# When background sums are queued: two weight units behind their split, the second half with the second group, none ahead of a half-step's last tile

## The chip, the cores and the metric

The kernel runs on one core of one Trainium2 chip. The metric is the device time of one execution in microseconds (us), as the median of several runs. A profile of one execution shows every instruction of the core's engines: TensorE (PE; its weight loads are listed as PEld), VectorE (DVE), ScalarE (ACT), GpSimd (POOL) and SyncE (SP), which issues most of the DMAs.

## What is computed

Two layers of an encoder trunk over 512 tokens of 1024 features, in f32. Each layer has three half-steps, so six follow one another, numbered s = 0 to 5: an FFN (s = 0, 3), a mixer of three parallel head groups (s = 1, 4), and a second FFN (s = 2, 5). Each is conditioned on one vector c:

```python
c_act = jax.nn.silu(c)
for l in range(DEPTH):
    mod = (c_act @ ada_w[l] + ada_b[l]).reshape(b, N_SUB, 3, 1, D_MODEL)

    h = modulate(x, mod[:, 0, 0], mod[:, 0, 1])          # x * (1 + scale) + shift
    y = swiglu_ffn(h, ffn1_w_in[l], ffn1_w_out[l])       # (silu(gate) * up) @ w_out, d_ff 2816
    x = layer_norm(ALPHA * x + 0.5 * mod[:, 0, 2] * y, ln_g[l, 0], ln_b[l, 0])
    ...
```

The change is about `c_act @ ada_w`: for each half-step a shift, a scale and a gate of 1024 numbers, each the product of one vector of 1024 with a 1024 x 1024 block of weights (4 MB). Shift and scale of a half-step are needed when its input is made, the gate when its output is added to x.

## The kernel before, in words

**The main work.** x lies in four tiles of 128 tokens (`xt`). For the matmuls its normalised and modulated transpose lies as features by tokens in `hT`, split in a high part `hh` and a low part `hl`, so that three fast matmuls (`mm3`, L106: low x high, high x low, high x high) stand for one f32 matmul. Weights are split in the same way: SP loads a unit of 1 MB (`ri`, `ro`), ACT copies it to the high part (`hi`, `ho`), and DVE subtracts for the low part (`li`, `lo`).

`ffn` (L659) goes through 11 pairs of 256 features in two groups, 0 to 5 and 6 to 10. A pair `jp` needs two weight units, gate and up; each is followed by a call of `tick()`. Then come its 4 x 8 x 3 = 96 matmuls into four PSUM banks (`pf`), then silu, product and split into `ah`, `al`. After a group, `out_proj` (L710) multiplies its 12 or 10 slices with the output weights, in two halves of 512 columns (`h`), each with up to three weight units and a `tick()` behind each; all ticks of a half precede its matmuls (`po`). The second group's second half goes tile by tile: 30 matmuls for token tile 0, `fold` (adds the gated result to x), layer norm, then `drain()` (L391), then tile 1, and from there on `modulate(s + 1, t - 1)` for the tile before. So tiles 0 to 2 of the next half-step's input are made there. The last tile, 3, is made inside the next half-step: in an FFN, `last_tile` is called behind the second of eight groups of matmuls of the first pair (`POS`, L681), which run first on tokens 0 to 255 and then on 256 to 511. Its `hl` is two DVE instructions, one for each half of the features.

**The background work** makes gates, scales and shifts with generators that are advanced by ticks. One part (a gate, a scale or a shift) consists of:

- `ada_acc` (L227): eight loads of rows (`ra`, 512 KB, from two buffers, `adap`), each multiplied by a number per partition and accumulated on DVE in two halves of 512 (`acc`). The first accumulation is ordered behind `ln_done`, which is the `hl` of the tile that was modulated last when the generator reaches that line. After the eighth a `TICK` ends the current tick.
- `acc_split` (L245): ACT makes the high part `gh` and DVE the low part `gl`. Both halves of `gl` lie in one of the two row buffers.
- a `TICK`, then the sum over partitions: two matmuls with a matrix of ones for each half (`acc_sum`, L256), into `pg` for a gate and `pm` for scale and shift. For a gate the bias is added on DVE; for scale and shift DVE picks the diagonal (`dg`) and adds it up (`sums`). After scale and shift, `mod_finish` makes `modA` and `modB` in five short DVE instructions.

`tick` (L381) adds the pace to a credit and advances the first pending generator once for each unit of credit, until a `TICK` ends it. The pace is 2.7 where `begin` gets four generators (s = 0, 3: this half-step's gate, scale and shift of the next, the next one's gate, scale and shift of the one after) and 1.3 else (s = 2, 5). The mixer starts no background work.

**What sets the order.** Each engine runs its own queue in order. The queues are arranged when the program is built by a planner: it takes what its own timing model holds ready, and among that what comes first in the program. Orders written by hand (`after`, `issue_after`) bind two instructions of one engine.

Of the kernel before, what the change touches and what calls it, by code (L numbers as in the profile page):

```python
# [30 lines left out]
PAD_W = 16  # L31
POS = 1
TICK = object()
CR = (2.7, 1.3)
WSZ = 1024

C_Z, C_XS, C_B, C_C, C_DT = 0, 512, 1024, 1280, 1536
# [31 lines left out]
def trunk(ctx, tc, x, c, ln_in_g, ln_in_b, ada_w, ada_b, ffn1_w_in, ffn1_w_out,  # L69
# [24 lines left out]
    def pa(shape, name):  # L94
        return psa.tile(shape, F32, tag="a", name=name)

    def pb(shape, name):
        return psb.tile(shape, F32, tag="b", name=name)

    def slot(shape, dt, name):  # L100
        return lp.tile(shape, dt, tag="s", name=name)

    def tmp(shape, name, dt=F32):
        return tp.tile(shape, dt, tag="t", name=name)
# [122 lines left out]
    def ada_acc(l, col):  # L227

        w = ada_w[l].rearrange("(p k) f -> p k f", k=KD)
        acc = [slot([P, 512], F32, f"acc{l}_{col}_{h}") for h in range(2)]  # L230
        for k in range(KD):
            raw = adap.tile([P, D], F32, tag="ra", name=f"ra{l}_{col}_{k}")
            sp.dma_start(raw, w[:, k, col:col + D])
            for h in range(2):
                rk = raw[:, h * 512:(h + 1) * 512]
                if k == 0:
                    after(dve.tensor_scalar(acc[h], rk, cT[:, 0:1], None, op0=ALU.mult), ln_done[0])
                else:
                    dve.scalar_tensor_tensor(acc[h], rk, cT[:, k:k + 1], acc[h],
                                             op0=ALU.mult, op1=ALU.add)  # L240
            yield acc
        yield TICK
        yield acc

    def acc_split(acc):  # L245

        parts = []
        los = adap.tile([P, 2, 512], F32R, tag="ra", name="gl")
        for h in range(2):
            hi, lo = tmp([P, 512], "gh", F32R), los[:, h]  # L250
            act.activation(hi, acc[h], AF.Copy)
            dve.tensor_tensor(lo, acc[h], hi.bitcast(F32), ALU.subtract)
            parts.append((hi, lo))
        return parts

    def acc_sum(ps, hi, lo):  # L256

        pe.matmul(ps, onesr, hi, start=True, stop=False)
        pe.matmul(ps, onesr, lo, start=False, stop=True)

    def new_mod(s):
        modA[s] = const.tile([P, KD], F32, name=f"modA{s}")
        modB[s] = const.tile([P, KD], F32, name=f"modB{s}")
# [19 lines left out]
    def ada_ss(s):  # L283
        l, j = divmod(s, 3)
        new_mod(s)
        pres = []
        for which in (1, 0):
            acc = None
            for a in ada_acc(l, (j * 3 + which) * D):
                acc = acc if a is TICK else a  # L290
                yield a
            sums = sm.tile([P, KD], F32, tag=f"sums{which}", name=f"sums{which}", bufs=1)
            parts = acc_split(acc)
            yield TICK
            for h in range(2):
                ps = pb([P, 4, P], f"pm{s}_{which}_{h}")
                acc_sum(ps, *parts[h])
                dg = tmp([P, 4, P], "dg")
                dve.tensor_tensor(dg, ps, ident[:, None, :].to_broadcast([P, 4, P]), ALU.mult)
                dve.tensor_reduce(sums[:, h * 4:h * 4 + 4], dg, axis=AX.X, op=ALU.add)  # L300
            pres.append(sums)
        mod_finish(s, 0, KD, *pres)
# [42 lines left out]
    def ada_gate(s):  # L345
        l, j = divmod(s, 3)
        col = (j * 3 + 2) * D
        gate = [slot([P, 512], F32, f"gate{s}_{h}") for h in range(2)]
        for h in range(2):
            sp.dma_start(gate[h], ada_b[l, col + h * 512:col + h * 512 + 512].partition_broadcast(P))  # L350
        acc = None
        for a in ada_acc(l, col):
            acc = acc if a is TICK else a
            yield a
        parts = acc_split(acc)
        yield TICK
        for h in range(2):
            ps = pb([P, 512], f"pg{s}_{h}")
            acc_sum(ps, *parts[h])
            dve.tensor_tensor(gate[h], ps, gate[h], ALU.add)  # L360
        gates[s] = gate
# [9 lines left out]
    pending = []  # L371

    credit = [0.0, 0.0]

    def begin(*gens):

        pending.extend(gens)
        credit[0] = 0.0
        credit[1] = len(pending) and CR[0] if len(gens) > 2 else CR[1]

    def tick():  # L381
        credit[0] += credit[1]
        while pending and credit[0] >= 1:
            try:
                if next(pending[0]) is TICK:
                    break
                credit[0] -= 1
            except StopIteration:
                pending.pop(0)
# [27 lines left out]
    def cols_unit(w, c0, name, prev=None):  # L417

        v = load(w, c0, 0, KD, 256, name)
        return [split(v[:, :, j * P:(j + 1) * P], f"{name}_{j}", prev) for j in range(2)]  # L420
# [235 lines left out]
    def by_token(ah, al):  # L656
        return lambda t: (ah[:, t * P:(t + 1) * P], al[:, t * P:(t + 1) * P])

    def ffn(s, w_in, w_out):  # L659
        for gi, grp in enumerate((range(0, 6), range(6, NPAIR))):  # L660
            acts = []
            for jp in grp:
                units, banks = [], []
                for which in range(2):
                    if s > 0 or jp > 0:
                        units.append(next_unit if (s, jp, which) == (0, 1, 0) else cols_unit(w_in, which * DFF + jp * 256, f"i{s}_{jp}_{which}", ln_done[0] if s > 0 and jp == 1 else None))
                        banks.append([pa([P, T], f"pf{s}_{jp}_{which}_{j}") for j in range(2)])
                    tick()
                if s == 0 and jp == 0:
                    banks, order = first_banks, []  # L670
                elif jp == 0:
                    order = [(0, KD, a, a + 256, j, which) for a in (0, 256) for which in range(2) for j in range(2)]
                else:
                    order = [(0, KD, 0, T, j, which) for j in range(2) for which in range(2)]
                for i, (ka, kb, a, b, j, which) in enumerate(order):
                    wh, wl = units[which][j]
                    for k in range(ka, kb):
                        mm3(banks[which][j][:, a:b], wh[:, k, :], wl[:, k, :],
                            hT[0][:, k, a:b], hT[1][:, k, a:b], k == 0, k == KD - 1)
                    if jp == 0 and i == POS:  # L680
                        last_tile[0](mm_last[0])  # L681
                for j in range(2):
                    sg = tmp([P, T], "sg")
                    act.activation(sg, banks[0][j], AF.Silu)
                    af = tmp([P, T], "af")
                    dve.tensor_tensor(af, sg, banks[1][j], ALU.mult)
                    ah = slot([P, T], F32R, f"ah{s}_{jp}_{j}")
                    al = slot([P, T], F32R, f"al{s}_{jp}_{j}")
                    act_last[0] = act.activation(ah, af, AF.Copy)
                    dve.tensor_tensor(al, af, ah.bitcast(F32), ALU.subtract)  # L690
                    acts.append(by_token(ah, al))
                if 0 < jp <= NT:
                    x_affine(s, jp - 1)
                if jp == 1:
                    if s == 0:
                        masks()
                        rows = [(vT[0], rows_v(0)), (vT[1], rows_v(1)), (lnT, rows_ln())]
                        small_loads(0)
                        small_loads(1)
                if s == 0 and jp == 3:  # L700
                    for r in rows:
                        columns(*r)
                    neg_a()
            last = gi == 1
            if last:
                if s == 5:
                    ln_vectors(6)
            out_proj(s, w_out, grp[0] * 256, acts, True, not last, last)
# [469 lines left out]
    for s in range(6):  # L1178
        l, j = divmod(s, 3)
        if j == 0:  # L1180
            begin(ada_gate(s), ada_ss(s + 1), ada_gate(s + 1), ada_ss(s + 2))
            ffn(s, ffn1_w_in[l], ffn1_w_out[l])
        elif j == 1:
            mixer(s, l)
        else:
            begin(ada_gate(s), *([ada_ss(s + 1)] if s < 5 else []))
            ffn(s, ffn2_w_in[l], ffn2_w_out[l])


# [29 lines left out]
```

## Time and profile before

| what | value |
|---|---|
| median of 3 runs | 1988.9 us (1988.61 to 1991.4) |
| the profiled execution | 1988.45 us, of which its span is 1986.7 us |
| granted TensorE clock, mean | 0.997 of full speed |
| instructions | 23052, of which 9230 matmuls |
| DMA | 263.95 MB, mean 133 GB/s |
| row loads of the background work (`ra`) | 128 of 512 KB, 4.6 us from issue to landing (median) |

Times in the profile's rows are counted from the span's start. A row of the timeline gives start, duration, engine, line, operation and the tiles it writes and reads; a bracket behind it is the time for which its engine stood idle ahead of it, and what ended that. Nearly all rows name L52: that is the wrapper through which PE, DVE and ACT instructions are issued, so they are told apart by their tiles. Ends of matmuls are modelled, their starts are measured. A row of the waits gives who waited for whom: total us, times, longest.

### The profile page before, as it was taken

The page shows a single profiled execution, that of the slowest core. Times are in us where ns is not written, and L with a number is a line of the kernel's source. Part 1 is how long each engine was busy: PE and PEld are TensorE (multiplying, and loading weights), DVE is VectorE, ACT ScalarE, POOL GpSimd, SP SyncE. Part 2 cuts the span into 40 slices and gives each one's busy share as a digit, 9 for nine tenths or more (in the row PEclk, how much of TensorE's full clock was granted, in tenths as well). Part 3 has the DMA queues.
Part 4 walks back from the last instruction along what each step waited for, and adds up shares of the span by engine and source line. Part 5 has one row for each costly group of instructions (what it writes and reads, how often), then busy time and mean ns, then how long its engine had stood idle before and what let it go on. Part 6 is the DMA issues. An engine that isn't in the chain of part 4 may idle for free.

```text
span 1986.7 us, 23052 instructions
## 1 busy us (share of the span) xinstructions
PE 1937.8 (98%) x9230; PEld 1616.3 (81%) x9230; DVE 1206.4 (61%) x1804; ACT 705.8 (36%) x1126; POOL 97.8 (5%) x126
## 2 busy tenths in 40 slices
PE   5999999999999999999999999999999999999998
PEld 4787888888878888888888788788888788888887
DVE  8886753477867655643478757436786676333336
ACT  3432222264575332132253222323546643222220
POOL 0100000012100000000000000000140000000000
PEclk9999999999999999999999999999999999999999
DMA  9675542143222544432256656322322243223321
GB/s 329 213 256 193 186 163 96 54 128 106 85 75 82 173 140 167 138 128 83 98 170 201 222 165 227 102 89 65 119 84 96 75 141 129 92 91 121 106 85 43
DMA packets 176730, 263.95 MB, mean 133 GB/s; under 512 B 9806, under 2 KB 124628, under 8 KB 176624
## 3 DMA queue, kind: packets, MB, share of 16 engines
q1 hardware_dynamic: 174000, 254.98, 38.7%
q0 software_dynamic: 2624, 7.52, 1.3%
q8 instruction: 72, 1.18, 0.2%
q14 instruction: 34, 0.28, 0.0%
HBM read 260.37 MB, written 2.10 MB: 132 GB/s over the span
## 4 chain that ended last, share of the span: by engine, by line
PE 81%; DVE 8%; DMA 6%; ACT 3%; issue 1%; POOL 0%; SPq 0%; POOLq 0%; DVEq 0%; ACTq 0%
PE pf L52 39%; PE po L52 26%; DMA ra<-in_ada_w_dram 5%; DVE acc L52 2%; PE pz L52 2%; PE pjm4x L52 1%; PE pjm1x L52 1%; ACT hf L52 1%; DVE li L52 1%; DVE af L52 1%; PE py L52 1%; DVE x L52 1%; PE pfo L52 1%; PE pjm1c L52 1%; PE pjm1k L52 1%
## 5 line engine op out<-in xcount | busy, mean ns | idle before, releaser
L52 PE MATMUL pf<-hl,hi 128*128 128x512 f32 (+1 forms) x1504 | 567.1, 377 | 7.5 <-DVE hl L52 7.5
L52 PE MATMUL pf<-hh,li 128*128 128x512 f32 (+1 forms) x1504 | 567.6, 377 | 1.5 <-DVE li L52 1.2
L52 PE MATMUL pf<-hh,hi 128*128 128x512 f32 (+1 forms) x1504 | 566.4, 377 | 0.0
L52 PEld LDWEIGHTS pf<-hl,hi 128*128 128x128 f32 x1504 | 284.7, 189 | 59.9 <-DVE hl L52 8.8
L52 PEld LDWEIGHTS pf<-hh,li 128*128 128x128 f32 x1504 | 284.7, 189 | 53.0 <-DVE li L52 1.7
L52 PEld LDWEIGHTS pf<-hh,hi 128*128 128x128 f32 x1504 | 284.6, 189 | 50.6
L52 DVE TENSOR_TENSOR li<-ri,hi 128x1024 fp32r<-128x1024 f32 x176 | 214.0, 1221 | 181.6 <-ACT hi L52 181.3
L52 ACT ACTIVATE hi<-ri 128x1024 fp32r<-128x1024 f32 x176 | 185.7, 1060 | 350.4 <-PE pf L52 214.4
L52 PE MATMUL po<-ho,al 128*128 128x512 f32 (+1 forms) x704 | 273.3, 388 | 0.4 <-DVE af L52 0.4
L52 PE MATMUL po<-lo,ah 128*128 128x512 f32 (+1 forms) x704 | 272.9, 388 | 0.0
L52 PE MATMUL po<-ho,ah 128*128 128x512 f32 (+1 forms) x704 | 272.6, 388 | 0.0
L52 DVE TENSOR_TENSOR lo<-ro,ho 128x1024 fp32r<-128x1024 f32 x104 | 127.1, 1223 | 206.8 <-ACT ho L52 206.6
L52 DVE SCALAR_TENSOR_TENSOR acc<-ra,cT,acc 128x512 f32<-128x512 f32 x224 | 157.6, 746 | 76.8 <-DMA ra<-in_ada_w_dram 76.3
L52 ACT ACTIVATE ho<-ro 128x1024 fp32r<-128x1024 f32 x104 | 110.0, 1058 | 257.6 <-PE po L52 156.2
L52 ACT ACTIVATE sg<-pf 128x512 f32<-128x512 f32 x88 | 52.5, 596 | 294.0 <-PE pf L52 293.9
L52 PEld LDWEIGHTS po<-ho,al 128*128 128x128 f32 x704 | 132.2, 188 | 27.9 <-DVE af L52 0.8
L52 PEld LDWEIGHTS po<-lo,ah 128*128 128x128 f32 x704 | 132.2, 188 | 27.0
L52 PEld LDWEIGHTS po<-ho,ah 128*128 128x128 f32 x704 | 132.2, 188 | 26.9
L52 DVE TENSOR_TENSOR af<-sg,pf 128x512 f32<-128x512 f32 x88 | 60.1, 684 | 145.8 <-PE pf L52 145.8
L52 ACT ACTIVATE hf<-ptr,modB,modA 128x128 f32<-128x128 f32 (+1 forms) x168 | 66.9, 489 | 98.1 <-PE ptr L52 84.5
L450 POOL TENSOR_TENSOR rs<-ve,mhalf 128x1 f32<-128x1 f32 x28 | 17.2, 616 | 1354.1 <-DVE ve L52 1352.7
L52 ACT ACTIVATE ah<-af 128x512 fp32r<-128x512 f32 x88 | 54.5, 619 | 29.9 <-DVE af L52 28.8
(407 smaller groups left out, 2361.9 us busy)
## 6 DMA issues: line engine op xcount, KB each, us to landing
ri<-in_ffn_w_in_dram SPq DMA_DIRECT2D x88, 1024.0 KB, 5.0
ra<-in_ada_w_dram SPq DMA_DIRECT2D x128, 512.0 KB, 4.6
ro<-in_ffn_w_out_dram SPq DMA_DIRECT2D x40, 1024.0 KB, 4.9
ro<-in_mix_w_out_dram SPq DMA_DIRECT2D x8, 1024.0 KB, 5.0
rf<-in_ada_w_dram SPq DMA_DIRECT2D x8, 512.0 KB, 7.3
ro<-in_ffn_w_out_dram SPq DMA_DIRECT2D x8, 512.0 KB, 3.6
rf<-in_ada_w_dram SPq DMA_DIRECT2D x16, 192.0 KB, 6.2
gate<-in_ada_b_dram SPq DMA_DIRECT2D x12, 256.0 KB, 5.7
```

The lines of the kernel that those rows point to most:

```text
L52: ins = f(*a, **k)
L450: pool.tensor_tensor(rs, ve, mhalf[:, 0:1], ALU.pow)
```

## The change

1. In `ada_ss` and `ada_gate` a second `TICK` stands between the split and the sum, so that the sum is queued at the second tick behind the split, and not at the first.
2. `begin` gets the pace as an argument, and the pace of s = 0 and 3 is 2.0 for 2.7. The next half-step's gate, and scale and shift of the one after, are no longer pending from the start of the half-step: `ffn` takes them as `later` and appends them when its second group begins.
3. In the first pair of a half-step with s > 0, the two calls of `tick` are left out. Each adds half the pace to the credit, and one `tick` is called behind `last_tile`.
4. With nothing pending, `tick` sets the credit to zero.

```diff
-CR = (2.7, 1.3)
+CR = (2.0, 1.3)
...
             parts = acc_split(acc)
             yield TICK
+            yield TICK
             for h in range(2):
                 ps = pb([P, 4, P], f"pm{s}_{which}_{h}")
...
         parts = acc_split(acc)
         yield TICK
+        yield TICK
         for h in range(2):
             ps = pb([P, 512], f"pg{s}_{h}")
...
-    def begin(*gens):
+    def begin(pace, *gens):
 
         pending.extend(gens)
         credit[0] = 0.0
-        credit[1] = len(pending) and CR[0] if len(gens) > 2 else CR[1]
+        credit[1] = pace
 
     def tick():
         credit[0] += credit[1]
+        if not pending:
+            credit[0] = 0.0
         while pending and credit[0] >= 1:
...
-    def ffn(s, w_in, w_out):
+    def ffn(s, w_in, w_out, *later):
         for gi, grp in enumerate((range(0, 6), range(6, NPAIR))):
             acts = []
+            if gi == 1:
+                pending.extend(later)
             for jp in grp:
...
-                    tick()
+                    if s == 0 or jp > 0:
+                        tick()
+                    else:
+                        credit[0] += credit[1] / 2
...
                     if jp == 0 and i == POS:
                         last_tile[0](mm_last[0])
+                        tick()
...
         if j == 0:
-            begin(ada_gate(s), ada_ss(s + 1), ada_gate(s + 1), ada_ss(s + 2))
-            ffn(s, ffn1_w_in[l], ffn1_w_out[l])
+            begin(CR[0], ada_gate(s), ada_ss(s + 1))
+            ffn(s, ffn1_w_in[l], ffn1_w_out[l], ada_gate(s + 1), ada_ss(s + 2))
...
         else:
-            begin(ada_gate(s), *([ada_ss(s + 1)] if s < 5 else []))
+            begin(CR[1], ada_gate(s), *([ada_ss(s + 1)] if s < 5 else []))
             ffn(s, ffn2_w_in[l], ffn2_w_out[l])
```

With the generators counted through tick by tick: before, in s = 0 and 3, the six parts are split and summed (split, then sum; "out" is an output projection, its half and weight unit) at pair 2, 2; pair 3, pair 4; pair 5, 5; out of group one, first half, second half; the same projection's second half, pair 6; pair 7, 7. After: pair 2, 3; pair 4, 5; out of group one, first half, second half; pair 8, 9; pair 10, out of group two, first half; the same projection's second half, `drain`. In s = 2 and 5 the splits stay where they were, and each sum moves on by one tick. In s = 2, 3 and 5 the first loads and accumulations move from ahead of the last tile to behind it: two, five and two before it become two, four and two behind it.

## The prediction

> **What bounds the kernel now.** I read the page first, then TensorE's own waits, then the timeline around each of them.
>
> ```profile
> span 1986.7 us, 23052 instructions
> PE 1937.8 (98%) x9230; PEld 1616.3 (81%) x9230; DVE 1206.4 (61%) x1804; ACT 705.8 (36%) x1126; POOL 97.8 (5%) x126
> ...
> PE 81%; DVE 8%; DMA 6%; ACT 3%; issue 1%; POOL 0%; SPq 0%; POOLq 0%; DVEq 0%; ACTq 0%
> ```
>
> TensorE (PE) is busy 98% of the span and is 81% of the chain that ended last. No other engine is near a bound, so the question is only where PE stands still. PE's waits from 60 us on (what is waited for; total us, times, longest):
>
> ```profile
> PE pf L52 <- DVE hl L52: 7.3, 3, 2.7
> PE pm L52 <- ACT gh L52: 6.2, 4, 2.3
> PE pyt L52 <- DVE xd L52: 2.1, 4, 0.7
> PE pg L52 <- DVE gl L52: 0.4, 1, 0.4
> PE po L52 <- DVE af L52: 0.4, 1, 0.4
> PE pv L52 <- DVE hl L52: 0.3, 2, 0.2
> ```
>
> That is 16.7 us, of which 13.9 (7.3 + 6.2 + 0.4) belong to the two things the change touches: the sums over partitions (`pm`, `pg`) and the last tile's `hl`. The start-up before 60 us is left as it is.
>
> The longest wait of a sum:
>
> ```profile
> 1240.81 0.39 PE L52 MATMUL pf<-hl,hi 128*128 128x512 f32 x1
> ...
> 1241.04 0.39 PE L52 MATMUL pf<-hh,hi 128*128 128x512 f32 x1
> ...
> 1242.16 1.41 DVE L52 SCALAR_TENSOR_TENSOR acc<-ra,cT,acc 128x512 f32<-128x512 f32 x2
> ...
> 1243.00 1.24 ACT L52 ACTIVATE gh<-acc 128x512 fp32r<-128x512 f32 x2
> ...
> 1243.68 0.51 PE L52 MATMUL pm<-gh,onesr 128*128 128x512 f32 x1 [2.26 <-ACT gh L52]
> ```
>
> The sum stands in PE's queue before its `gh` exists, and the FFN matmuls behind it wait too. Steady matmuls start every 0.23 us (1240.81 to 1241.04) though a row shows 0.39, so an end is drawn 0.16 us late and a stall is 0.16 us longer than its bracket: 1243.68 - 1241.04 - 0.23 = 2.41, not 2.26.
>
> The last tile, where half-step 2 begins (DVE rows, one ACT row, one PE row):
>
> ```profile
> 640.87 0.92 DVE L52 TENSOR_SCALAR acc<-ra,cT 128x512 f32<-128x512 f32 x2
> 641.71 1.40 DVE L52 SCALAR_TENSOR_TENSOR acc<-ra,cT,acc 128x512 f32<-128x512 f32 x2
> 644.00 0.69 DVE L52 TENSOR_TENSOR hl<-hf,hh 128x512 fp32r<-128x512 f32 x1 [0.89 <-ACT hh L52]
> 649.73 1.42 DVE L52 SCALAR_TENSOR_TENSOR acc<-ra,cT,acc 128x512 f32<-128x512 f32 x2 [5.03 <-DMA ra<-in_ada_w_dram]
> 651.06 0.68 DVE L52 TENSOR_TENSOR hl<-hf,hh 128x512 fp32r<-128x512 f32 x1
> ```
> ```profile
> 645.05 0.63 ACT L52 ACTIVATE hh<-hf 128x512 fp32r<-128x512 f32 x1
> ```
> ```profile
> 649.02 0.28 PE L52 MATMUL pf<-hh,li 128*128 128x256 f32 x1
> 651.80 0.58 PE L52 MATMUL pf<-hl,hi 128*128 128x256 f32 x1 [2.50 <-DVE hl L52]
> ```
>
> `hh` was done at 645.68, but VectorE (DVE) stood at an accumulation whose weight rows landed only at 649.7; `hl`, queued behind it, came at 651.74. The same shape stands at half-steps 3 and 5.
>
> After such a stall PE's granted clock may drop (window; its length, PE busy and count, PEld, DVE, ACT, POOL; clock):
>
> ```profile
> 652.00:655.00 3.00, 3.00 (x15) 3.00 (x16) 3.00 (x4) 0.44 (x1) 0.00 (x0) 0.50 0.60 180
> ...
> 1017.00:1020.00 3.00, 3.00 (x27) 3.00 (x27) 0.00 (x0) 0.00 (x0) 0.00 (x0) 1.00 0.84 318
> ...
> 1023.00:1027.00 4.00, 4.00 (x24) 4.00 (x24) 4.00 (x6) 1.54 (x2) 0.00 (x0) 0.60 0.81 239
> ...
> 1629.00:1633.00 4.00, 3.89 (x32) 3.89 (x33) 4.00 (x6) 1.55 (x2) 0.00 (x0) 1.00 0.54 154
> ```
>
> At full clock 27 such matmuls take 3.00 us. The 15 and the 24 would have taken 1.67 and 2.67 instead of 3.00 and 4.00: 1.3 us each, 1.4 with the window's edges. After the third stall the clock stayed at 1.00.
>
> **The change, part by part.** Counted through the code, 16 parts (a gate, a scale or a shift: 8 row loads, 16 accumulations, 2 splits, 4 sum matmuls) run in the six half-steps. Before, one tick lies between split and sum. Where both ticks precede the same pair's matmuls, no PE work stands between: 6 parts, and 5 of them are the 5 waits above (`pm` 4, `pg` 1). The other 10 have a block of at least 96 matmuls (22 us) between, and none of them waited.
>
> 1. *Sums two ticks behind the split.* Now 14 parts have such a block; no new instruction appears. The tightest old sum of this kind:
>
> ```profile
> 235.10 1.35 DVE L52 TENSOR_TENSOR gl<-acc,gh 128x512 fp32r<-128x512 f32 x2
> ```
> ```profile
> 239.25 0.39 PE L52 MATMUL pm<-gh,onesr 128*128 128x512 f32 x1
> ```
>
> `gl` is done 2.8 us ahead, with parts following each other as fast as they could; the slower pace adds room. Removed: 6.2 + 0.4 + 5 x 0.16 = **7.4 us**. The price: `gl` keeps one of the two row buffers until its sum has run, so the next part's loads begin later. That is step 3's matter.
>
> 2. *No tick ahead of a last tile.* The first accumulation is now emitted after the last tile's `modulate` and is ordered behind its `hl`; the later ones need the first one's result. So none can stand ahead, and `hl` goes at 645.7, 2.6 us before PE wanted it (649.02 + 0.12, less its 0.7). Behind it come two accumulations (0.92 + 1.40) and the next pair's `li`, which PE wants only when the pair in hand ends, 192 matmuls of 0.12 us after its start; that hides them. The gate's two bias loads and the row loads move behind the last tile on SP's queue too. Removed: 7.3 + 3 x 0.16 + 2 x 1.4 = **10.6 us**.
>
> 3. *Second half with the second group, pace 2.0 for 2.7.* In half-steps 0 and 3 three parts (24 row loads of 512 KB, two bias loads) leave the first group for the second. They move past the first group's output weights on SP's queue; POOL's queue holds none of it. Three parts then have to fit in the second group, and the last sum falls to `drain`, behind output tile 0. Room in the second output projection, and the price of the parts:
>
> ```profile
> 351.00:378.50 27.50, 27.50 (x123) 22.78 (x122) 9.18 (x10) 5.82 (x6) 0.00 (x0) 1.00 0.28 84
> 378.50:385.30 6.80, 6.80 (x32) 5.63 (x31) 6.48 (x11) 0.88 (x1) 0.00 (x0) 1.00 0.01 1
> 385.30:392.20 6.90, 6.90 (x33) 5.64 (x32) 3.25 (x6) 0.00 (x0) 0.56 (x1) 1.00 0.19 42
> ```
> ```profile
> L52 DVE TENSOR_TENSOR dg<-pm,ident x20: 677/682/693, 127.1 to 1246.1; 128x512 f32<-128x512 f32 x20
> L52 DVE TENSOR_REDUCE sums<-dg x20: 671/676/679, 128.3 to 1247.3; 128x4 f32<-128x512 f32 x20
> L52 DVE SCALAR_TENSOR_TENSOR modA<-sums,vT x5: 156/159/160, 133.9 to 1226.4; 128x8 f32<-128x8 f32 x5
> ```
> ```profile
> 205.68 0.39 PE L52 MATMUL pg<-gh,onesr 128*128 128x512 f32 x1
> ```
> ```profile
> 234.43 1.29 ACT L52 ACTIVATE gh<-acc 128x512 fp32r<-128x512 f32 x2 [4.79 <-DVE acc L52]
> ```
> ```profile
> 265.99 1.23 ACT L52 ACTIVATE gh<-acc 128x512 fp32r<-128x512 f32 x2
> ```
>
> From one sum to the next `gh` took 28.8 us (205.68 to 234.43) and 26.7 (239.25 to 265.99). The last part starts where the output projection does (351) and its sum stands after 27.5 + 6.8 = 34.3 us, so by these rows `gh` is there at 378 to 380 and `gl` 1.4 us later if DVE is free. DVE is 6.48 of 6.80 busy just then with the folds of four tiles, so `gl` may slip to about 385: just in time. At the drain DVE gets 2 x 0.68 + 2 x 0.68 + 5 x 0.16 = 3.5 us more, in a stretch with 6.90 - 3.25 = 3.65 us free. That cover is thin, and without it the last tile's `hl`, already 0.3 us late at the mixer (`pv`), slips by as much. The rows do not show a sum at this place: bounds are 0 (all fits) and 3.5 + 1.4 us per turnover (no work fits, and `gl` waits besides). I take 1.0, near the lower end because both rows leave room; twice that is **2.0 us**.
>
> Nothing hidden should come free below that: the remaining waits (`pyt` 2.1, `po` 0.4) are of other work, and I leave 0.4 for `po`.
>
> Sum: -7.4 - 10.6 + 2.0 = -16.0 us. The profiled execution took 1988.45 us, so 1972.5; the median of the runs shown is 0.45 higher, so I forecast **1973**.
>
> **Rivals.**
>
> *The forecast* (chance 0.60): 1969 (nothing given back, `po` too) to 1977.
>
> *Order in the program isn't order on the engines* (0.12). The instruction planner already put the accumulation of 649.73, emitted after the last tile, ahead of its `hl`. If it also pulls the sums forward to where its own timing thinks `gh` ready, the 7.4 us stay. Only step 2 holds, by a real dependence: 1988.45 - 10.6 + 0.45 = 1978, and 1980 with step 3's price. Against it: the 10 old sums with a block between stood where the block ended, none earlier.
>
> *The drain takes back most* (0.15). If the chain takes some 40 us instead of 27 to 29, PE waits about 5 us at each drain and loses 1.4 of clock: 18.0 - 12.8 leaves 5, so 1984; with half of it, 1980. For it: parts are loaded beside the output weights, and two ticks later the buffer is freed later. Against it: DMA is 0.28 busy there, the old chains ran at more.
>
> *Slower* (0.05), the same place, with its price in full: if the held `gl` buffer left one row buffer for the loads, they would go one after the other.
>
> ```profile
> L52 DVE SCALAR_TENSOR_TENSOR acc<-ra,cT,acc x224: 733/746/754, 58.6 to 1646.4; 128x512 f32<-128x512 f32 x112
> ...
> DMA to landing us min/median/max: 3.3/4.6/8.2
> ```
>
> 8 x (4.6 + 2 x 0.75) = 49 us against 34.3: 15 us late at each drain, 30 in all, +2.8 of clock: 1988.9 - 18.0 + 32.8 = 2004. It ends slower than before from a chain of about 43 us on. Against it: the old chains of 27 to 29 us had a `gl` in that buffer as well.
>
> *The clock drop isn't the stall's* (0.08). The third stall (2.7 us, the longest) cost no clock, so the two drops may fall there for another reason and stay: 2.8 us less, 1976. [...]
>
> **How the numbers follow.** A measurement of this kernel can tell about 0.2% (4 us) from no change: under 1984.9 is faster, over 1992.9 slower. Forecast, order and clock (0.60 + 0.12 + 0.08) lie under 1984.9; of the drain's 0.15 I put 0.06 under it and 0.09 within; slower 0.05. So 0.86, 0.09, 0.05. The range runs from 1969 to 1982: it holds the forecast, order and clock, and leaves out the larger drain and the slower case.
>
> **What would show it.** Step 1: no `pm` or `pg` in PE's waits, and `gl` ended 5 us or more ahead of each sum but the two at the drains. Step 2: no `pf` waiting for `hl`, and clock 1.00 through the first 30 us of half-steps 2, 3 and 5. Step 3: at each drain, `pm` right behind tile 0's 30 matmuls with no wait, and `pv <- hl` at 0.3 us as now. I am wrong if `pm <- gh` or `gl` stands at the drains with more than 2 us, if weights (`li`, `lo`) begin to appear among PE's waits, or if PE is free of these waits and the span is still above 1980.

## The result, and the profile after

| | median | runs |
|---|---|---|
| before | 1990.15 us (1988.61 to 1991.45) | 4 |
| after | 1969.72 us (1968.32 to 1970.33) | 4 |

The ratio is 0.9894 with an interval of 0.9878 to 0.991: 20.4 us less. The forecast was 1973, in a range of 1969 to 1982, and the result lies 0.7 us above the lower end of it. The profiled execution took 1970.33 us, 18.1 less than that of before.

The page of the kernel after, its span, the busy time of each engine and the chain that ended last:

```profile
span 1968.5 us, 23071 instructions
...
PE 1933.6 (98%) x9230; PEld 1615.5 (82%) x9230; DVE 1204.3 (61%) x1804; ACT 705.4 (36%) x1126; POOL 97.8 (5%) x126
...
PE 94%; DVE 3%; ACT 2%; DMA 1%; POOL 0%; issue 0%; POOLq 0%; SPq 0%; DVEq 0%; ACTq 0%
```

The work is the same: 9230 matmuls, 1804 DVE instructions. In the chain PE's share rose from 81% to 94%, and that of the DMAs, on which it had come to rest when an accumulation waited for its rows, fell from 6% to 1%. TensorE's waits from 60 us on, in the kernel after (total us, times, longest):

```profile
PE pyt L52 <- DVE xd L52: 2.1, 4, 0.7
PE po L52 <- DVE af L52: 0.5, 1, 0.5
PE pv L52 <- DVE hl L52: 0.3, 2, 0.2
```

`pf <- hl`, `pm <- gh` and `pg <- gl`, 13.9 us together, are gone, and no line took their place. The last tile where half-step 2 begins (DVE's timeline, kernel after):

```profile
643.83 0.69 DVE L52 TENSOR_TENSOR hl<-hf,hh 128x512 fp32r<-128x512 f32 x1 [1.02 <-ACT hh L52]
644.44 0.88 DVE L52 TENSOR_SCALAR acc<-ra,cT 128x512 f32<-128x512 f32 x2
```

The first accumulation follows the second `hl`, where it had stood ahead of it. The first 30 us of half-steps 2, 3 and 5 (windows, kernel after; the clock is the number behind POOL's count):

```profile
632.00:662.00 30.00, 30.00 (x233) 29.02 (x232) 21.73 (x32) 17.48 (x32) 3.11 (x5) 1.00 0.70 222
1000.00:1030.00 30.00, 30.00 (x229) 28.96 (x228) 21.91 (x32) 16.35 (x31) 3.42 (x5) 1.00 0.80 255
1598.00:1628.00 30.00, 30.00 (x225) 28.80 (x224) 21.56 (x31) 17.03 (x30) 3.11 (x5) 1.00 0.72 229
```

PE is busy throughout, at full clock. The drain of half-step 0, where the last sum now stands (timelines of PE and of DVE, kernel after):

```profile
382.24 0.39 PE L52 MATMUL po<-ho,ah 128*128 128x512 f32 x1
382.46 0.39 PE L52 MATMUL pm<-gh,onesr 128*128 128x512 f32 x1
```
```profile
381.10 1.27 DVE L52 TENSOR_TENSOR gl<-acc,gh 128x512 fp32r<-128x512 f32 x2
```

`gl` was held behind the folds and ended at 382.37, 0.1 us before the first sum matmul. That one reads `gh`, which ended at 377.8; the two sum matmuls that read the halves of `gl` start at 382.69 and 383.15, 0.9 and 0.8 us after their halves were ready. So nothing waits, with 0.8 us to spare.

The profiled execution shows less gain than the medians because of its start. The first FFN matmuls and the transposes behind them, kernel before and kernel after (PE's timeline):

```profile
32.02 0.50 PE L52 MATMUL pf<-hh,li 128*128 128x512 f32 x1 [1.17 <-DVE li L52]
34.20 0.60 PE L52 MATMUL ptr<-ident,x 128*128 128x128 f32 x4
```
```profile
32.10 0.80 PE L52 MATMUL pf<-hh,li 128*128 128x512 f32 x1 [1.00 <-DVE li L52]
36.10 0.67 PE L52 MATMUL ptr<-ident,x 128*128 128x128 f32 x4
```

The same matmuls took 2.18 us before and 4.00 after, with rows of 0.80 for 0.50 us: 1.8 us, at a place that the change doesn't touch. The clock goes with it: its record begins, at full clock, at 30.54 us in the kernel before and at 36.24 in the kernel after, where matmuls from 32.69 to 36.10 start 0.43 us apart, against 0.23 in the kernel before (from 32.36 to 34.20). In a second profile of the changed kernel (`after_again`, below) it was 2.18 again, with steps of 0.23 there.

### The profile page after: what moved, and what is told of

Its sections match the earlier page's. It is cut to its first block, busy times and chain, and to the rows that moved or that the text cites. A ratio compares the mean times of both kernels' runs of the same rounds, so it can differ in the third digit from the quotient of the medians.

```text
span 1968.5 us, 23071 instructions
## 1 busy us (share of the span) xinstructions
PE 1933.6 (98%) x9230; PEld 1615.5 (82%) x9230; DVE 1204.3 (61%) x1804; ACT 705.4 (36%) x1126; POOL 97.8 (5%) x126
## 4 chain that ended last, share of the span: by engine, by line
PE 94%; DVE 3%; ACT 2%; DMA 1%; POOL 0%; issue 0%; POOLq 0%; SPq 0%; DVEq 0%; ACTq 0%
PE pf L52 48%; PE po L52 29%; PE pz L52 2%; PE pjm4x L52 1%; PE pjm1x L52 1%; PE ptr L52 1%; PE py L52 1%; DVE af L52 1%; PE pfo L52 1%; PE pjm1c L52 1%; PE pjm4k L52 1%; PE pjm1k L52 1%; PE pjm4c L52 1%; PE pjm1q L52 1%; PE pjm4q L52 1%; PE pjm4b L52 1%
```

## The experiments

The theory is that of the prediction: PE lost its time at two things, sums queued before their part was ready, and last tiles queued behind an accumulation; each part of the change takes away one of them. The rivals: the order in the program doesn't decide, the drain takes the gain back, the clock drops have another cause. Beside the first four kernels below, the kernel before took 1990.67 us (1985.35 to 2000.38, 23 runs); beside the next four, 1990.57 (1983.0 to 1998.01, 21 runs); beside the last three, 1991.38 (1987.0 to 1997.19, 13 runs). The ratios are to these.

### One part undone

`u_tick`, the changed kernel without the second `TICK`:

```diff
             yield TICK
-            yield TICK
             for h in range(2):
                 ps = pb([P, 4, P], f"pm{s}_{which}_{h}")
...
         yield TICK
-        yield TICK
         for h in range(2):
             ps = pb([P, 512], f"pg{s}_{h}")
```

> The changed kernel without the second TICK; pace, second half and last tile as changed. Counted by ticks, only the sums of the last parts (for half-steps 2 and 5) then stand in front of the same matmuls as their split, with 120 matmuls (27 us) since their first accumulation. Theory A (a sum waits only where less PE work lies between its part's first accumulation and itself than the 24 to 29 us that a part takes): no pm or pg wait but at these two, 0 to 3 us each, 1970 to 1976 us. Rival B (the slower pace alone makes gh early; the second TICK does nothing): as the changed kernel, 1970 us, no such wait. Rival C (the second TICK is what takes all five waits away): at least 7 us slower than the changed kernel, 1977 us, with four or more pm/pg waits.

Measured: 1976.89 us (1975.58 to 1978.53, 6 runs), ratio 0.993 [0.9909, 0.9951]: 7.2 above the 1969.72 of the changed kernel. PE's waits in it, and its timeline at the second output projection of half-step 0:

```profile
PE pm L52 <- ACT gh L52: 3.1, 2, 1.5
...
PE pm L52 <- DVE gl L52: 0.9, 1, 0.9
```
```profile
376.72 1.02 PE L52 MATMUL pm<-gh,onesr 128*128 128x512 f32 x2 [1.53 <-ACT gh L52]
...
381.19 0.50 PE L52 MATMUL pm<-gl,onesr 128*128 128x512 f32 x1 [0.89 <-DVE gl L52]
```

The waits stand at the last part of half-steps 0 and 3 alone. The sums that waited in pairs 2 and 5 in the kernel before no longer do, although split and sum are one tick apart here as they were there: the slower pace has moved them. So pace and second `TICK` share the work of the prediction's step 1. The places are those of theory A, but the time is 0.9 us above its range and at the 1977 of rival C: the steps at the sums are 5.4 us longer in all than in the changed kernel, and 1.7 us of clock were lost behind the second of the two (1343 us, shown in the last section). A had no term for the clock.

`u_last`, the changed kernel with the ticks ahead of the last tile as before:

```diff
-                    if s == 0 or jp > 0:
-                        tick()
-                    else:
-                        credit[0] += credit[1] / 2
+                    tick()
...
                         last_tile[0](mm_last[0])
-                        tick()
```

> The changed kernel with the ticks ahead of the last tile as before. Theory A: pf waits for hl at half-steps 2, 3 and 5, 2 to 3 us each, and the clock falls to about half for some 3 us behind two or three of them: 7 to 12 us slower than the changed kernel, 1977 to 1982 us; no sum waits. Rival (with the pace lower the accumulations no longer stand late in front of hl at half-step 3): two waits, about 5 to 8 us. Rival (the clock drop isn't the stall's): the waits come back but the clock stays at 1.00 behind all of them, 8 us.

Measured: 1978.35 us (1976.81 to 1983.58, 6 runs), ratio 0.9942 [0.9919, 0.9964]: 8.6 above the changed kernel. Its three stalls (PE's timeline), and 8 us of windows from each:

```profile
646.98 0.38 PE L52 MATMUL pf<-hl,hi 128*128 128x256 f32 x1 [1.30 <-DVE hl L52]
...
1015.66 0.39 PE L52 MATMUL pf<-hl,hi 128*128 128x256 f32 x1 [1.74 <-DVE hl L52]
...
1616.39 0.49 PE L52 MATMUL pf<-hl,hi 128*128 128x256 f32 x1 [2.50 <-DVE hl L52]
```
```profile
647.00:655.00 8.00, 8.00 (x67) 8.00 (x68) 7.12 (x8) 3.25 (x4) 0.00 (x0) 1.00 0.79 256
1016.00:1024.00 8.00, 8.00 (x69) 8.00 (x68) 7.16 (x10) 2.60 (x3) 0.00 (x0) 1.00 0.81 259
1616.00:1624.00 8.00, 7.61 (x51) 7.61 (x52) 6.92 (x9) 2.60 (x3) 0.00 (x0) 0.79 0.75 234
```

The `hl` waits are back at the same three places, and no sum waits. At the third place the clock held in the kernel before, behind a bracket of 2.7 us, and fell here behind 2.50; at the first two it fell before (2.5 and 2.1) and holds here (1.30 and 1.74). The drop goes with the stall and not with the place.

### One part alone

`o_last`, the kernel before with the last-tile part alone:

```diff
-                    tick()
+                    if s == 0 or jp > 0:
+                        tick()
+                    else:
+                        credit[0] += credit[1] / 2
...
                         last_tile[0](mm_last[0])
+                        tick()
```

> The kernel before with the last-tile part of the change alone. Theory A: the three waits of pf for hl go, with their clock drops, and the four or five waits of sums stay (6 to 8 us in all): 10.6 us faster than before, 1978 to 1980 us, clock 1.00 through the first 30 us of half-steps 2, 3 and 5. Rival (the clock drop isn't the stall's): clock near 0.5 for some 3 us at the same places, only 8 us faster.

Measured: 1981.8 us (1976.94 to 1987.89, 12 runs), ratio 0.9958 [0.9941, 0.9976]: 8.9 below the kernel before, 1.8 above the expected range. Its profile is of the fastest run (1976.94), at a mean granted clock of 0.998, where that of the kernel before had 0.997. Of the waits named above only those of sums are left in it, 5.2 us for the 6 to 8 expected:

```profile
PE pm L52 <- ACT gh L52: 4.8, 4, 1.6
...
PE pg L52 <- DVE gl L52: 0.4, 1, 0.4
```

`o_half`, the kernel before with the pace of 2.0 and the second half queued with the second group (and the credit set to zero when nothing is pending), one `TICK`, ticks ahead of the last tile:

```diff
-CR = (2.7, 1.3)
+CR = (2.0, 1.3)
...
+            if gi == 1:
+                pending.extend(later)
...
-            begin(ada_gate(s), ada_ss(s + 1), ada_gate(s + 1), ada_ss(s + 2))
-            ffn(s, ffn1_w_in[l], ffn1_w_out[l])
+            begin(CR[0], ada_gate(s), ada_ss(s + 1))
+            ffn(s, ffn1_w_in[l], ffn1_w_out[l], ada_gate(s + 1), ada_ss(s + 2))
```

> The kernel before with the pace of 2.0 and the second half queued with the second group, without the second TICK and without the last-tile part. Theory A: the three hl waits stay with their clock drops; of the five sum waits those of half-steps 0 and 3's first groups go, those of the last parts may stay with 0 to 3 us each: 2 to 8 us faster than before, 1981 to 1987 us. Rival C (only the second TICK helps the sums): no faster than before, 1988 us. Rival (the held buffer and the drain cost something): slower than before.

Measured: 1986.24 us (1985.31 to 1990.08, 12 runs), ratio 0.9976 [0.9964, 0.9989]: 4.4 below the kernel before. PE's waits:

```profile
PE pf L52 <- DVE hl L52: 6.0, 3, 2.5
PE pm L52 <- ACT gh L52: 3.1, 2, 1.5
PE pm L52 <- DVE gl L52: 2.4, 2, 1.4
```

The sums of pairs 2 and 5 have stopped waiting here too; that of pair 7 has moved to the second output projection and waits there. With 4.4 for this part, 7.2 for the second `TICK` and 8.6 for the last tile the three come to 20.2 us, against 20.4 in all (by the ratios 4.8, 7.2 and 9.6, 21.6 against 21.1): they add up within 0.5 us, and nothing was given back. The second `TICK` on the old pace and the old halves was not run, so what it does without the pace is seen in `pace27` alone, below.

### The second half and the pace

`after_again`, the changed kernel again, beside the following ones:

> The changed kernel once more, on the chip that runs the three below: 1968 to 1971 us. If tight sums and last tiles are also what spreads the runs of before (they depend on when a load lands), its runs lie within some 3 us; if the chip spreads them, within 10 us as those of before do.

Measured: 1969.53 us (1969.12 to 1969.99, 4 runs), ratio 0.9894 [0.9872, 0.9917].

`nolater`, the changed kernel with all four generators pending from the start, so that the last sum comes in the second output projection's first half and none at the drain:

```diff
-            begin(CR[0], ada_gate(s), ada_ss(s + 1))
-            ffn(s, ffn1_w_in[l], ffn1_w_out[l], ada_gate(s + 1), ada_ss(s + 2))
+            begin(CR[0], ada_gate(s), ada_ss(s + 1), ada_gate(s + 1), ada_ss(s + 2))
+            ffn(s, ffn1_w_in[l], ffn1_w_out[l])
```

> The changed kernel with all four generators pending from the start of the half-step, as before, at the pace of 2.0 and with two TICKs: no sum falls to the drain, each has at least 96 matmuls behind its split and 192 since its first accumulation. Theory (the drain costs nothing): as the changed kernel, 1969 to 1971 us, no pm or pg wait. Rival (the sums at the drains cost about 1 us each, as the prediction took): 2 us faster than the changed kernel, 1967.5 us.

Measured: 1969.85 us (1969.52 to 1970.89, 5 runs), ratio 0.9896 [0.9873, 0.9918]; no `pm`, `pg` or `hl` among its waits. The sum at the drain costs nothing, and queueing the second half later brings nothing either. What of this part counts is the pace.

`pace16`, the changed kernel with a slower pace (`CR = (1.6, 1.3)` for `(2.0, 1.3)`):

> The changed kernel with a pace of 1.6: the last parts of half-steps 0 and 3 begin only in the second output projection's second half, 30 matmuls (7 us) ahead of the drain, and their split and sum fall to the drain. Theory (the rival of the drain, its price one to one): a part takes 24 to 29 us, so scale and shift of the next half-step come 17 to 22 us behind the drain, the four tiles of its input wait for them, and PE stands still for 8 to 20 us at each of the two turnovers, with clock lost behind it: 1988 to 2012 us, slower than before at the upper end. Rival (the planner hides it behind the 90 matmuls of tiles 1 to 3 and the mixer): 1970 to 1976 us.

Measured: 1994.23 us (1992.61 to 1995.42, 11 runs), ratio 1.0016 [1.0003, 1.0028]: slower than before, if by little. Two waits carry it, one at each drain (PE's timeline; then SP's issues at the first of them):

```profile
392.15 0.79 PE L52 MATMUL pm<-gh,onesr 128*128 128x512 f32 x1 [9.63 <-ACT gh L52]
...
1367.99 0.79 PE L52 MATMUL pm<-gh,onesr 128*128 128x512 f32 x1 [9.48 <-ACT gh L52]
```
```profile
373.70 12.53 SPq L233 DMA_DIRECT2D ra<-in_ada_w_dram  x4
```

The part's first accumulation ran at 351.7 us, as early as in the changed kernel (351.3), but its last four row loads are issued only from 373.7 on: fewer ticks are left for them, and `drain` runs the rest at once. So `gh` comes 40 us after the first accumulation, and the sum, in PE's queue behind tile 0, holds tiles 1 to 3. So the time lies in the expected range, but not by the way that was expected: the part did not begin late, it was stretched. That is the prediction's *slower* rival, with its place, its sign and nearly its length of chain (some 43 us), made long not by the buffers but by the ticks that hand out the loads.

`pace27`, the changed kernel at the old pace (`CR = (2.7, 1.3)`):

> The changed kernel with the old pace of 2.7 in half-steps 0 and 3. Two TICKs, second half with the second group; but by the ticks the last parts' split and sum fall ahead of the same matmuls again, 96 matmuls (22 us) after their first accumulation. Theory (22 us is less than the 24 to 29 us that a part takes): pm waits at these two sums, 1 to 3 us each, none elsewhere: 1972 to 1977 us. Rival (two TICKs are enough at any pace): 1970 us, no pm wait.

Measured: 1997.29 us (1994.75 to 1999.87, 11 runs), ratio 1.0034 [1.0021, 1.0047]. Both the size and the places of the expectation were wrong: it looked for waits at the last part of each half-step, and they stand at the second (PE's timeline), with the clock behind them (windows):

```profile
129.43 1.46 PE L52 MATMUL pm<-gh,onesr 128*128 128x512 f32 x2 [4.45 <-ACT gh L52]
...
335.39 0.79 PE L52 MATMUL pm<-gh,onesr 128*128 128x512 f32 x1 [4.00 <-ACT gh L52]
...
1108.20 0.57 PE L52 MATMUL pm<-gh,onesr 128*128 128x512 f32 x1 [4.49 <-ACT gh L52]
...
1313.36 0.80 PE L52 MATMUL pm<-gh,onesr 128*128 128x512 f32 x1 [4.38 <-ACT gh L52]
```
```profile
129.40:137.00 7.60, 7.57 (x20) 5.83 (x21) 7.60 (x18) 4.42 (x8) 0.00 (x0) 0.59 0.48 140
335.00:343.00 8.00, 7.61 (x22) 5.77 (x23) 8.00 (x14) 3.16 (x6) 0.00 (x0) 0.66 0.67 197
```

At each of these four places 96 matmuls lie between split and sum, which by the prediction's count was enough. (At the last parts, where the waits were expected, `gh` ended 0.05 and 0.06 us ahead of its sum, 23.0 and 21.7 us after the part's first accumulation.) Counted through the code, the 96 are also all that lies between the part's *first accumulation* and its sum: at this pace eight loads and the split fall into one pair. 96 x 0.227 = 22 us, and `gh` came 24 to 25 us after the first accumulation. The same count fits the kernel before: its four `pm` waits are the four parts with 96 matmuls from the first accumulation to the sum, and the two with 144 (33 us) had `gl` 2.8 and 3.7 us early. (Its fifth wait, `pg` with 0.4 at 85 us, is of another kind: `gh` ended at 81.86, in time for its sum at 81.91, but `gl` ran only at 84.36, behind other work in DVE's queue.) In the changed kernel each part but the two at the drains has 192 or more (44 us), and `gl` is early by 11.9 us or more.

`pace27_t3` gives those parts more without touching the pace: the kernel `pace27` with a third `TICK` behind the second, in `ada_ss` and `ada_gate`.

```diff
             yield TICK
             yield TICK
+            yield TICK
             for h in range(2):
```

> The changed kernel at pace 2.7 with a third TICK between split and sum. Theory (what counts is PE work from a part's first accumulation to its sum, not the pace): the four parts whose sum had 96 matmuls behind the first accumulation get a block more (192, 44 us, against 24 to 29 us needed), so the waits of 4.0 to 4.5 us at 129, 335, 1108 and 1313 us are gone; the last part of a half-step sums at the drain behind 120 matmuls (27 us) and may wait 0 to 2 us there; 1969 to 1976. Rival (the faster pace costs by itself, through loads that crowd the weights or slow matmuls): the sum waits are gone but the time stays at 1985 or more. Second rival (the last part moves the wait to the drain): 4 us or more at each drain, 1980 to 1990.

Measured: 1976.37 us (1976.04 to 1977.61, 4 runs), ratio 0.9935 [0.992, 0.995]. No sum waits any more, so it is not the old pace by itself that makes them wait: some 20 us came back. The third `TICK` lengthens the way from the split and that from the first accumulation alike. That the second of the two decides follows beside it from the changed kernel, where at pairs 2 to 3 and 4 to 5 there are also 96 matmuls from split to sum, 192 from the first accumulation, and no wait. The 1976 of the theory was just missed. What is left over the changed kernel has a new name (PE's waits; then DVE's timeline there):

```profile
PE po L52 <- DVE dg L52: 3.5, 1, 3.5
PE po L52 <- DVE af L52: 2.5, 2, 1.4
```
```profile
801.01 0.75 DVE L52 SCALAR_TENSOR_TENSOR acc<-ra,cT,acc 128x512 f32<-128x512 f32 x1 [3.47 <-DMA ra<-in_ada_w_dram]
...
807.62 1.28 DVE L52 TENSOR_TENSOR dg<-pm,ident 128x512 f32<-128x512 f32 x2
```

DVE stood for 3.47 us at an accumulation whose rows had not landed, and `dg`, which empties `pm` and stands behind the folds there, came late by as much; an output matmul waited for it. It is the last tile's disease at another place: a load's wait on an engine that serves PE.

`pace27_gl` asks why a part takes that long. It is `pace27` with `gl` in two short-lived tiles, so that both row buffers stay with the loads:

```diff
-        los = adap.tile([P, 2, 512], F32R, tag="ra", name="gl")
...
-            hi, lo = tmp([P, 512], "gh", F32R), los[:, h]
+            hi, lo = tmp([P, 512], "gh", F32R), tmp([P, 512], "gl", F32R)
```

> The changed kernel at pace 2.7, with gl in two short-lived tiles instead of one of the two row buffers. At pace 2.7 alone the kernel took 1997.3 us, with four waits of 4.0 to 4.5 us for gh at 129, 335, 1108 and 1313 us, where 96 matmuls (22 us) run between a part's first accumulation and its sum and gh came 24.3 to 24.7 us after that start. Theory (the held buffer makes a part long: its loads begin only when the sum before has run): the loads of the next part begin at the split, the first accumulation comes some 4 us earlier, gh is there at or before the sum; the four waits fall to 0 to 1.5 us each and the time to 1970 to 1980. Rival (a part is bound by eight loads through two buffers, whatever gl holds): the first accumulation does not move ahead of the sum before, the waits stay within 1 us of 4.0 to 4.5 and the time at 1993 to 1998.

Measured: 1992.41 us (1988.53 to 1994.93, 10 runs), ratio 1.0002 [0.999, 1.0014]. PE's waits:

```profile
PE pm L52 <- ACT gh L52: 10.7, 6, 3.1
...
PE pm L52 <- DVE gl L52: 1.7, 4, 0.8
```

Neither side was right. The four long waits shrank from 4.0 to 4.5 us to 1.7 to 3.1, so the held buffer does cost, 1.4 to 2.4 us of each wait, while six waits of 0.2 to 0.9 came up beside them; and the first accumulation still came behind the sum before, at 105.5 in place of 104.8, since the generator reaches the next part's first load only once it has emitted the sum. That the rest of a part's length, still 21.6 us and more, is eight loads through two buffers beside the weights is likely, and not shown by a run.

`after_gl` is the changed kernel with the same edit:

> The changed kernel with gl in two short-lived tiles instead of one of the two row buffers. Theory (no sum waits any more in the changed kernel, and the drain's sum is just in time without a wait): 1968.5 to 1970.5, the same as the changed kernel; only the slack at the drains grows, from 0.1 us between gl and its sum to 2 us or more, if the held buffer is what delays the part's first load. Rival (the held buffer delays something that PE pays for without a wait by name): 1966 or less.

Measured: 1970.74 us (1968.79 to 1971.62, 4 runs), ratio 0.9904 [0.989, 0.9919], the changed kernel's time. Where nothing waits, a shorter part is worth nothing. The slack at the drain did not grow, against the expectation: from a half of `gl` to the sum matmul that reads it it is 0.9 and 0.3 us (0.9 and 0.8 in the changed kernel). The accumulations were done at 370.8, and DVE's folds hold `gl` there until 379.6, not the loads.

No version tried beats the changed kernel.

## Why the prediction was right

**Step 1, sums two ticks behind the split: -7.4 us, measured about -9.5.** The five stalls went; from start to start they were 7.5 us, as forecast. Another 2.0 us went that the prediction had not counted. The wait of 1.53 us in the kernel before shows them (PE's timeline):

```profile
1126.80 0.50 PE L52 MATMUL pm<-gh,onesr 128*128 128x512 f32 x1 [1.53 <-ACT gh L52]
1127.13 0.40 PE L52 MATMUL pf<-hh,hi 128*128 128x512 f32 x1
1127.52 0.50 PE L52 MATMUL pm<-gh,onesr 128*128 128x512 f32 x1
1127.99 0.51 PE L52 MATMUL pm<-gl,onesr 128*128 128x512 f32 x1
1128.34 0.39 PE L52 MATMUL pf<-hh,li 128*128 128x512 f32 x1
```

The matmuls at 1126.80 and 1127.99, each behind a pause, show 0.50 and 0.51 for the usual 0.39 or 0.40, and the next ones start 0.33 and 0.35 us later instead of 0.23 (1127.13, 1128.34). Two short stalls have no bracket here, as an end is drawn late: the second `gh` and the first `gl` came 0.16 and 0.25 us behind the steady step (1127.52, 1127.99). All steps at sums, start to start, less 0.227 each, make 9.7 us before (7.48 in the five stalls, 2.21 in the rest) and 0.21 after. The mechanism was right and its size 2 us short.

Its reason was only half right. "A block between split and sum" fitted the kernel before, but `pace27` has one and waits 4 us. What decides is PE's work between a part's first accumulation and its sum, against the 21 to 28 us that a part needs from there. So the pace, which the prediction booked as a cost in step 3, is the other half of what removes these waits: `u_tick` shows it working with one `TICK`, `pace27` shows two `TICK`s failing without it.

**Step 2, no tick ahead of a last tile: -10.6 us, measured 10.9 in the trace and 8.6 and 8.9 by the runs.** The three stalls were 7.8 us from start to start, and 3.1 were lost behind two of them; all of it is gone. Undone, the part costs 8.6: the stalls that come back are shorter, 1.5, 1.9 and 2.7 us, only one of them costs clock (1.6), and `po <- af` took 1.2 more, which has no tie to this part that a run shows. `hl` goes first by the real dependence that the prediction named, and `li` behind the accumulations made nobody wait.

**Step 3, second half with the second group: +2.0 us, measured 0.** This term was mis-sized. "Just in time" was right, with 0.8 us to spare, and `pv <- hl` stayed at 0.3; the 1.0 us per drain did not come, and `nolater` agrees. The cover that the prediction called thin held, and `pace16` shows what lies behind it: 9.5 us at each drain.

**The sum.** 9.5 + 10.9 = 20.4 us out of the profiled execution of before, nothing back. The two profiled executions differ by 18.1, or 19.9 with the 1.8 of the start, so 0.5 is not accounted for; that the medians differ by just 20.4 is chance, as the median of the kernel before was 1988.9 to 1991.38 from set to set. The forecast of 16.0 was low by 2 at the sums and by 2 at the drain. It is luck that the range held: 20.4 off the 1988.9 that the forecast started from is 1968.5, below its lower end.

**The rivals.** *Order in the program*: fell; the sums stood behind the tick where they were emitted. *The drain takes back most*: did not happen at this pace. *Slower*: did not happen either, but `pace16` and `pace27` show that 0.4 less or 0.7 more of pace turns the gain into a loss of 3 and 7 us (ratios 1.0016 and 1.0034); 0.05 was little for a change whose outcome hangs so closely on one number. *The clock drop isn't the stall's*: fell. The drops left with the stalls, and in `u_last` one came where before there was none. Why the longest stall cost none, no run shows.

## What to carry to other kernels

When background work is queued by hand ahead of an engine that takes its queue in order (as PE did: the FFN matmuls behind the sum of 1243.68 stood its 2.26 us with it), count the main engine's work from the *first* step of a part (its first load's use) to the instruction that needs the part, and compare it with the part's own length. The distance between the last two steps says little, and a faster pace can shorten the first while it leaves the second as it is. Keep instructions that wait for loads out of the queue ahead of anything that the main engine will want soon; and where all waits are gone, measure the pace on both sides, because the optimum can lie between two losses.

## What the runs showed of the hardware

**Behind some stalls the clock was lower, behind others not.** Two of the three `hl` stalls of the kernel before (PE's timeline), then 8 us of windows from each of its four longest stalls on; the first and the third of these windows belong to the `hl` stall of 651.80 and to the sum of 1243.68:

```profile
1022.48 0.39 PE L52 MATMUL pf<-hl,hi 128*128 128x256 f32 x1 [2.13 <-DVE hl L52]
...
1629.11 0.39 PE L52 MATMUL pf<-hl,hi 128*128 128x256 f32 x1 [2.68 <-DVE hl L52]
```
```profile
651.00:659.00 8.00, 7.20 (x47) 7.20 (x48) 6.94 (x10) 2.60 (x3) 0.00 (x0) 0.79 0.70 217
1022.00:1030.00 8.00, 7.52 (x50) 7.53 (x51) 6.80 (x10) 2.60 (x3) 0.00 (x0) 0.79 0.77 216
1243.00:1251.00 8.00, 7.32 (x32) 5.97 (x33) 7.36 (x12) 2.78 (x4) 0.00 (x0) 1.00 0.07 18
1629.00:1637.00 8.00, 7.89 (x65) 7.89 (x66) 7.25 (x9) 3.02 (x4) 0.00 (x0) 1.00 0.78 250
```

From start to start, less the steady step, these stalls are 2.66, 2.29, 2.42 and 2.84 us long. At the first two the clock record has 0.50 for 3.41 us each time (from 651.76 and from 1023.82), and the matmuls of 256 columns start 0.21 us apart instead of 0.12, which makes some 1.5 us each; at the other two it stays at 1.00. So it does at the three of 1.3 to 1.7 us (152.48, 266.67, 1126.80). In `u_last` the stall of 2.50 us (its bracket, as in what follows) has 0.79 in the 8 us from it on and those of 1.30 and 1.74 have 1.00. In `u_tick` two stalls of nearly the same length differ: the window of that at 376.72, 1.53 us long, has 1.00, and that of the other 0.79 (window):

```profile
1343.00:1351.00 8.00, 7.58 (x25) 5.86 (x26) 7.62 (x14) 0.87 (x2) 0.00 (x0) 0.79 0.01 2
```

In the three windows taken of `pace27`, stalls of 4.45, 4.00 and 4.49 us have 0.59, 0.66 and 0.79, or 3.1, 2.7 and 1.7 us of clock; the one of 9.63 in `pace16` has 0.64, or 2.9: more than twice the stall, and no larger loss. So these runs give no length from which on a stall costs clock.

**The runs of the kernel with the waits lay further apart.** The kernel before lay between 1985.35 and 2000.38 us in 23 runs, the changed one between 1969.12 and 1969.99 in four (`after_again`). Beside these four, the 21 runs of the kernel before go from 1983.0 at a granted clock of 0.999 to 1998.01 at 0.995, while the four all have 0.999. By estimate, a clock lower by 0.004 over 1990 us is 8 us, so the clock is about half of that spread of 15 us; that the rest is the waits themselves is likely, and no run shows it.
